# Low parts of the first stage's weight tiles: formed on GpSimd instead of VectorE

## The chip, the cores and the metric

The kernel runs on one core of a Trainium2 chip. The core has a matrix engine (TensorE, PE in the profile; its weight loads are PEld), a vector engine (VectorE, DVE), an activation engine (ScalarE, ACT), a general engine (GpSimd, POOL) and a queue engine for transfers (SyncE, SP). Each engine works through its own list of instructions in order and waits on semaphores for the others. TensorE reads from the on-chip memory SBUF and writes to the accumulators in PSUM. The metric is the time of one execution on the device in microseconds; a time is a median over runs.

## The reference

One sequence of 1024 frames with 1024 channels goes through two layers. All inputs and outputs are float32.

```
layer 0:  h = rmsnorm(x);  proj = h @ w_in                (1024 x 3328)
          14 column tiles -> RWKV-7 time mixing, 8 heads of 64 (a scan over time)
          12 column tiles -> chunked band attention, 8 heads of 64 (q, k, v)
          x += concat(y_rwkv, y_att) @ w_out
          x += square(relu(rmsnorm(x) @ up0)) @ dn0       (1024 x 4096, 4096 x 1024)
layer 1:  x += conformer_conv(rmsnorm(x))                 (pw1, GLU, causal conv of width 31,
                                                           layer norm, swish, pw2)
          x += square(relu(rmsnorm(x) @ up1)) @ dn1
output:   rmsnorm(x)
```

## The kernel before

**Products in two parts.** TensorE's fast format for float32 operands (`float32r`) keeps fewer digits than float32. So each operand is split: a high part, which is the value rounded to that format, and a low part, which is what is left. A dense product is the sum of three: high weight by high activation, high weight by low activation, low weight by high activation (lines 263, 264 and 265). ScalarE forms the high part by a copy, VectorE the low part by a subtraction of the high part from the raw value.

**Weight tiles.** `weight_part` (line 201) does this for weights. It takes a raw tile `wr` of 128 x 512 values (four blocks of 128 rows by 128 columns), loads it with a transfer on SyncE's queue (line 203), rounds it into `wh` on ScalarE (line 207) and subtracts into `wl` on VectorE (line 208). `wr` has four buffers. `wh` and `wl` have four each in the first stage (pool `wp1`) and eight each afterwards (pool `wp2`). One column tile of a product, with 1024 rows of weights, is two such parts (`weights`, line 211), and each part serves four blocks of rows, 12 matmuls of 512 columns. The value columns of the input projection (line 352) use parts of two row blocks by 256 columns: for each pair of column tiles four parts are made, and for each of four groups of frames all four are used one after the other.

**Stages.** The sequence is worked on in two halves of 512 frames. The first stage (everything before `wide[0] = True`) has: the input projection of half 0; then, mixed with one another, the scan and the attention of half 0 and the input projection of half 1; then the scan and the attention of half 1, mixed with the output projection and the feed-forward block (`up0`, `dn0`) of half 0. The second stage (after `wide[0] = True`) has the convolution of half 0, the rest of layer 0 for half 1, and the rest of layer 1 for both halves. `wide[0]` is False in the first stage and True in the second; it also makes `gemm` work on two column tiles at a time.

**Order.** The program names priorities: "support" first (loading and splitting of weights and activations, and taking results out of PSUM), then "mixer" (the scan), "attn" (the attention) and "dense" (the large matmuls). A planner at build time goes through all instructions with costs of its own, and for every engine puts the ready instruction of the highest priority next. The result is one fixed list for each engine. A change of an instruction's engine makes the planner plan anew, so other instructions can change places too. On the chip each list is worked through strictly in order.

**VectorE in the first stage.** Beside the weights' low parts it takes results out of PSUM, forms low parts of activations, and does most of the scan: among other things a triangular inversion in 16 steps of a product (line 584, two operands in SBUF) and a sum (line 587), with a detour through DRAM (`msc` to `nb`, `xsc` to `xdt`). It also does the attention's bias, maximum and scaling (lines 799 to 808).

**GpSimd before.** It sets small tiles to constants, copies a few small tiles (`dc` at line 496; the convolution's edge at lines 928 and 932), and issues transfers: stores of the projections (`pd`, `ph`, `pl`, `vd`; lines 342, 343, 345 and 371), of the mixers' outputs (`yd`; lines 719 and 828), of the half's state (`xd`, line 841), and the spreading of the bias rows (line 1055). An issue waits in GpSimd's list until the data to be stored is there.

Of the kernel before, what the change touches and what calls it, by code (L numbers as in the profile page):

```python
# [8 lines left out]
F32 = mybir.dt.float32  # L9
F32R = mybir.dt.float32r  # L10
AF = mybir.ActivationFunctionType
ALU = mybir.AluOpType
# [49 lines left out]
def encoder_trunk(ctx: ExitStack, tc: tile.TileContext, x, vecs, consts, ext, w2a2, g2, w_in, w_out,  # L62
                  up0, dn0, pw1, pw2, up1, dn1, out):
    nc = tc.nc
# [10 lines left out]
    wide = [False]  # L75
# [125 lines left out]
    def weight_part(src, n):  # L201
        raw = wpool.tile([P, KH, P], F32, tag="wr", name="wr", bufs=4)
        nc.sync.dma_start(raw[:].rearrange("p a b -> p (a b)").rearrange("p (k n) -> p k n", n=n),
                          src.rearrange("(k p) n -> p k n", p=P))
        hi = wb[0].tile([P, KH, P], F32R, tag="wh", name="wh")
        lo = wb[0].tile([P, KH, P], F32R, tag="wl", name="wl")
        nc.scalar.copy(hi[:], raw[:])  # L207
        nc.vector.tensor_tensor(out=lo[:], in0=raw[:], in1=hi[:].bitcast(F32), op=ALU.subtract)  # L208
        return hi, lo

    def weights(w, row0, m):
        return [weight_part(w[row0 + k0 * P : row0 + (k0 + KH) * P, P * m : P * m + P], P) for k0 in range(0, KT, KH)]
# [115 lines left out]
    def w_in_gemm(h, rhs, st, first=()):  # L328
# [19 lines left out]
        for n0 in range(V0 * P, V0 * P + RW, 2 * P):  # L348
            parts = []
            with boost():  # L350
                for k0 in range(0, KT, 2):
                    parts.append(weight_part(w_in[k0 * P : (k0 + 2) * P, n0 : n0 + 2 * P], 2 * P))
            for t in range(4):
                if t % 2 == 0:
                    q = psum("d")
                cs = slice(t % 2 * 2 * P, (t % 2 + 1) * 2 * P)
                ts = slice(t * P, (t + 1) * P)
                with At("dense"):
                    for k in range(KT):
                        xh, xl = rhs[k]  # L360
                        hi, lo = (a[:].rearrange("p a b -> p (a b)")[:, k % 2 * 2 * P : (k % 2 + 1) * 2 * P] for a in parts[k // 2])
                        nc.tensor.matmul(q[:, cs], xh[:, ts], hi, start=(k == 0), stop=False)
                        nc.tensor.matmul(q[:, cs], xl[:, ts], hi, start=False, stop=False)
                        nc.tensor.matmul(q[:, cs], xh[:, ts], lo, start=False, stop=(k == KT - 1))
                with boost():
                    if t % 2 == 0:
                        s = tmp("t1")
                    nc.scalar.activation(s[:, cs], q[:, cs], AF.Copy, scale=st.part[1][:, t : t + 1])
                    if t % 2:
                        r0 = h * T + (t - 1) * P  # L370
                        nc.gpsimd.dma_start(vd[r0 : r0 + 2 * P, n0 - V0 * P : n0 - V0 * P + 2 * P].rearrange("(a p) c -> p a c", p=P),
                                            s[:].rearrange("p (a c) -> p a c", a=2))
# [655 lines left out]
    with banks(d=2, w=2, v=1, c=1, a=2), tc.tile_pool(name="lop", bufs=1) as lop, tc.tile_pool(name="wp1", bufs=4) as wb[0]:  # L1028
# [5 lines left out]
        with tc.tile_pool(name="xrp", bufs=4, reuse_waits="tile") as xrp:  # L1034
            with boost():
                xa, ra, sa, first = load_x(0, xrp)
                for i, s in enumerate((slice(0, C), slice(C, P))):
                    raw = xrp.tile([P, RW], F32, tag=f"lr{i}", name="lr", bufs=1)
# [134 lines left out]
```

## Time and profile before

| what | us |
|---|---|
| median of three runs | 2561.08 (2558.75 to 2570.02) |
| the profiled execution's own time | 2570.09 |
| its span, first to last instruction | 2568.2 |
| its mean granted TensorE clock | 0.978 |
| TensorE busy (matmuls) | 2480.4 |
| VectorE busy | 1848.3 |
| ScalarE busy | 1143.9 |
| GpSimd busy | 111.6 |

All views in this document are of one profiled execution for each kernel. Times in them are counted from the first instruction. In a group's row stand the line of the program, the engine, the operation, the tile written and those read, the shape, the number of instructions, then their busy time in all, the mean duration of one in ns, and the idle time of the engine just before them with what ended it. In a row of the waits stand who waited, for whom, the time in all, how often, and the longest one. In a row on a single line of the program the durations are least, median and greatest. The chain of waits is followed back from the last instruction: at each step to what released it, or else to the instruction before it on its engine.

### The profile page before, as it was taken

The page shows a single profiled execution, that of the slowest core. Times are in us where ns is not written, and L with a number is a line of the kernel's source. Part 1 is how long each engine was busy: PE and PEld are TensorE (multiplying, and loading weights), DVE is VectorE, ACT ScalarE, POOL GpSimd, SP SyncE. Part 2 cuts the span into 40 slices and gives each one's busy share as a digit, 9 for nine tenths or more (in the row PEclk, how much of TensorE's full clock was granted, in tenths as well). Part 3 has the DMA queues.
Part 4 walks back from the last instruction along what each step waited for, and adds up shares of the span by engine and source line. Part 5 has one row for each costly group of instructions (what it writes and reads, how often), then busy time and mean ns, then how long its engine had stood idle before and what let it go on. Part 6 is the DMA issues. An engine that isn't in the chain of part 4 may idle for free.

```text
span 2568.2 us, 37380 instructions
## 1 busy us (share of the span) xinstructions
PE 2480.4 (97%) x12892; PEld 1971.0 (77%) x12892; DVE 1848.3 (72%) x3948; ACT 1143.9 (45%) x2224; POOL 111.6 (4%) x285
## 2 busy tenths in 40 slices
PE   8888999989999999999999999999999999999998
PEld 6667666757676767788888888888888888888887
DVE  5677788658788888546999974679999465544444
ACT  5345545555556655444343333533423355423324
POOL 1011001110000000000100000000000000000000
PEclk9898999989899999999999999999999999999999
DMA  8544444444333332236333333433333335333332
GB/s 266 157 141 137 115 121 119 140 130 119 95 104 107 102 101 81 77 107 197 95 93 100 96 99 99 140 115 95 95 99 99 99 91 156 95 95 98 99 97 68
DMA packets 476462, 291.24 MB, mean 113 GB/s; under 512 B 40416, under 2 KB 453472, under 8 KB 476272
## 3 DMA queue, kind: packets, MB, share of 16 engines
q1 hardware_dynamic: 466080, 258.11, 35.1%
q0 software_dynamic: 9152, 29.36, 3.3%
q8 instruction: 102, 1.67, 0.3%
q10 hardware_dynamic: 1040, 1.38, 0.2%
q14 instruction: 88, 0.72, 0.1%
HBM read 254.12 MB, written 37.77 MB: 114 GB/s over the span
## 4 chain that ended last, share of the span: by engine, by line
PE 82%; DVE 7%; DMA 6%; issue 3%; ACT 1%; SPq 0%; POOL 0%; ACTq 0%; DVEq 0%; POOLq 0%
PE d L264 23%; PE d L263 23%; PE d L265 23%; DMA nb<-msc 3%; DVE wl L208 1%; PE w L549 1%; PE a L824 1%; DVE pr L584 1%; DMA wr<-in_w_in_dram 1%; PE a L817 1%; PE c L665 1%; PE a L795 1%; DVE xi L587 1%; PE c L670 1%; DMA pt<-pd 1%
## 5 line engine op out<-in xcount | busy, mean ns | idle before, releaser
L207 ACT CAST wh<-wr 128x512 fp32r<-128x512 f32 x744 | 460.7, 621 | 988.9 <-PE d L264 897.2
L263 PE MATMUL d<-xh,wh 128*128 128x512 f32 x1872 | 748.4, 400 | 6.1 <-ACT xh L153 4.2
L264 PE MATMUL d<-xl,wh 128*128 128x512 f32 x1872 | 746.6, 399 | 0.8 <-DVE xl L154 0.4
L265 PE MATMUL d<-xh,wl 128*128 128x512 f32 x1872 | 746.3, 399 | 0.9 <-DVE wl L208 0.9
L208 DVE TENSOR_TENSOR wl<-wr,wh 128x512 fp32r<-128x512 f32 x744 | 501.9, 685 | 190.0 <-ACT wh L207 135.0
L263 PEld LDWEIGHTS d<-xh,wh 128*128 128x128 f32 x1872 | 356.9, 191 | 81.2 <-ACT xh L153 4.7
L264 PEld LDWEIGHTS d<-xl,wh 128*128 128x128 f32 x1872 | 356.5, 190 | 74.8 <-DVE xl L157 1.3
L265 PEld LDWEIGHTS d<-xh,wl 128*128 128x128 f32 x1872 | 356.5, 190 | 74.6 <-DVE wl L208 1.6
L263 PE MATMUL d<-mh,wh 128*128 128x512 f32 (+1 forms) x1040 | 405.9, 390 | 0.0
L264 PE MATMUL d<-ml,wh 128*128 128x512 f32 (+1 forms) x1040 | 405.2, 390 | 0.0
L265 PE MATMUL d<-mh,wl 128*128 128x512 f32 (+1 forms) x1040 | 404.9, 389 | 0.0
L947 DVE SCALAR_TENSOR_TENSOR cv<-u,dwt,cv 128x512 f32<-128x512 f32 x480 | 332.4, 746 | 0.7
L264 PEld LDWEIGHTS d<-ml,wh 128*128 128x128 f32 x1040 | 195.7, 188 | 38.9
L265 PEld LDWEIGHTS d<-mh,wl 128*128 128x128 f32 x1040 | 195.5, 188 | 39.1
L263 PEld LDWEIGHTS d<-mh,wh 128*128 128x128 f32 x1040 | 195.6, 188 | 38.4 <-issue 0.2
L846 DVE TENSOR_TENSOR x<-d,x 128x512 f32<-128x512 f32 (+1 forms) x146 | 97.6, 680 | 142.5 <-PE d L265 142.2
L888 DVE SCALAR_TENSOR_TENSOR t<-d,rstd 128x512 f32<-128x512 f32 x128 | 86.3, 686 | 101.2 <-PE d L265 98.1
L584 DVE TENSOR_TENSOR pr<-nb,xi 128x16 f32<-128x16 f32 (+15 forms) x256 | 101.0, 395 | 2.6
L894 DVE TENSOR_TENSOR ml<-t,mh 128x512 fp32r<-128x512 f32 x128 | 87.8, 688 | 13.5 <-ACT mh L892 10.9
L890 ACT ACTIVATE t<-t 128x512 f32<-128x512 f32 x128 | 80.1, 626 | 18.9 <-DVE t L888 18.4
L892 ACT ACTIVATE mh<-t 128x512 fp32r<-128x512 f32 x128 | 78.9, 616 | 0.0
L587 DVE TENSOR_REDUCE xi<-pr 128x8 f32<-128x16 f32 (+15 forms) x256 | 73.9, 289 | 2.4
(261 smaller groups left out, 2452.5 us busy)
## 6 DMA issues: line engine op xcount, KB each, us to landing
wr<-in_up_dram SPq DMA_DIRECT2D x256, 256.0 KB
wr<-in_dn_dram SPq DMA_DIRECT2D x256, 256.0 KB
wr<-in_w_in_dram SPq DMA_DIRECT2D x104, 256.0 KB
wr<-in_pw_dram SPq DMA_DIRECT2D x96, 256.0 KB
nb<-msc SPq DMA_DIRECT2D x16, 512.0 KB
wr<-in_w_out_dram SPq DMA_DIRECT2D x32, 256.0 KB
pd<-t POOLq DMA_DIRECT2D x28, 256.0 KB, 3.0
x<-xd SPq DMA_DIRECT2D x24, 256.0 KB
```

Source lines behind the costliest of these rows:

```text
L207: nc.scalar.copy(hi[:], raw[:])
L208: nc.vector.tensor_tensor(out=lo[:], in0=raw[:], in1=hi[:].bitcast(F32), op=ALU.subtract)
L263: nc.tensor.matmul(q[:, cols], hi, xh[:, cols], start=(k == 0), stop=False)
L264: nc.tensor.matmul(q[:, cols], hi, xl[:, cols], start=False, stop=False)
L265: nc.tensor.matmul(q[:, cols], lo, xh[:, cols], start=False, stop=(k == KT - 1))
L584: nc.vector.tensor_tensor(out=pr[:, :, :, 0:n], in0=pairs[:, r, :, 0:n].unsqueeze(2).to_broadcast([P, 2, 4, n]), in1=xi[:, :, 0:n].unsquee ...
L587: nc.vector.tensor_reduce(out=xi[:, :, n - 2 : n].rearrange("p j r -> p r j"), in_=pr[:, :, :, 0:n], op=ALU.add, axis=AX.X)
L846: nc.vector.tensor_tensor(out=xs[m][:, cols], in0=q[:, cols], in1=xs[m][:, cols], op=ALU.add)
L888: nc.vector.scalar_tensor_tensor(out=t[:], in0=q[:], scalar=0.0, in1=rstd[:], op0=ALU.max, op1=ALU.mult)
L890: nc.scalar.activation(sq[:], t[:], AF.Square)
L894: nc.vector.tensor_tensor(out=lo[:], in0=sq[:], in1=hi[:].bitcast(F32), op=ALU.subtract)
L947: nc.vector.scalar_tensor_tensor(out=c[:], in0=u[:, tap : tap + T], scalar=dw(tap), in1=c[:], op0=ALU.mult, op1=ALU.add)
```

## The change

In `weight_part` the subtraction that forms the low part is issued on GpSimd while `wide[0]` is False, that is for every weight tile of the first stage, and on VectorE afterwards, as before. Operands, shapes, buffers and priorities stay the same.

```diff
         nc.scalar.copy(hi[:], raw[:])
-        nc.vector.tensor_tensor(out=lo[:], in0=raw[:], in1=hi[:].bitcast(F32), op=ALU.subtract)
+        (nc.vector if wide[0] else nc.gpsimd).tensor_tensor(out=lo[:], in0=raw[:], in1=hi[:].bitcast(F32),
+                                                            op=ALU.subtract)
         return hi, lo
```

## The prediction

> **What bounds the kernel now.** I read the page first: its busy line, the slices and the costliest groups.
>
> ```profile
> span 2568.2 us, 37380 instructions
> PE 2480.4 (97%) x12892; PEld 1971.0 (77%) x12892; DVE 1848.3 (72%) x3948; ACT 1143.9 (45%) x2224; POOL 111.6 (4%) x285
> ...
> PE   8888999989999999999999999999999999999998
> ...
> DVE  5677788658788888546999974679999465544444
> ...
> L208 DVE TENSOR_TENSOR wl<-wr,wh 128x512 fp32r<-128x512 f32 x744 | 501.9, 685 | 190.0 <-ACT wh L207 135.0
> ...
> L584 DVE TENSOR_TENSOR pr<-nb,xi 128x16 f32<-128x16 f32 (+15 forms) x256 | 101.0, 395 | 2.6
> ```
>
> TensorE is the busy engine over the whole span, GpSimd is nearly empty, and VectorE is high in the first 18 slices, where the change lies. So I cut the first stage (to 1188 us, where the last of its dense work runs) into four stretches: all engines, then the low parts alone.
>
> ```profile
> 0.00:530.00 530.00, 483.98 (x2977) 363.24 (x2978) 385.61 (x1055) 260.06 (x571) 61.89 (x166) 0.94 0.50 148
> 530.00:580.00 50.00, 37.49 (x190) 26.30 (x189) 26.77 (x73) 24.07 (x55) 6.04 (x20) 0.80 0.48 145
> 580.00:1066.00 486.00, 465.47 (x3000) 344.16 (x2999) 396.23 (x1159) 273.48 (x596) 17.79 (x57) 0.98 0.36 98
> 1066.00:1188.00 122.00, 121.65 (x564) 99.87 (x563) 57.81 (x91) 46.68 (x78) 5.89 (x17) 1.00 0.42 123
> 0.00:1188.00 1188.00, 1108.58 (x6726) 833.57 (x6726) 866.41 (x2376) 604.30 (x1298) 91.61 (x260) 0.95 0.43 125
> ...
> 0.00:1188.00 1188.00, 169.11 (x249) 0.95 0.43 125
> ```
>
> After the length of a stretch come PE, PEld, DVE, ACT and POOL busy, the granted clock and the DMA. TensorE idles 1188 - 1108.6 = 79 us in this stage, 12.5 of it between 530 and 580, and 0.4 after 1066. Up to 1066 VectorE is busy 808.6 of 1066 us, or 76%. The last row is line 208 alone: 169 us of VectorE's 866. Its 249 instructions hold one of the next stage; by the code there are 104 + 16 + 64 + 64 = 248 (input projection, output projection, the two feed-forward matrices).
>
> Then the chain of waits of that stage, shares by line, and what TensorE waited for up to 1190 us (us in all, times, longest).
>
> ```profile
> by line: PE d L264 12.5%; PE d L263 12.4%; PE d L265 12.3%; issue 6.4%; DMA nb<-msc 6.0%; DVE wl L208 2.8%; PE w L549 2.4%; PE a L824 2.3%; DVE pr L584 2.2%; DMA wr<-in_w_in_dram 2.0%; PE a L817 1.8%; PE c L665 1.6%; PE a L795 1.5%; DVE xi
> ...
> PE v L612 <- DVE e L606: 14.3, 3, 6.3
> PE a L817 <- DVE pt L808: 7.1, 5, 3.8
> PE a L795 <- DVE yo L827: 5.9, 2, 3.5
> PE w L481 <- DVE xl L462: 5.8, 1, 5.8
> ...
> PE d L265 <- DVE wl L208: 0.9, 1, 0.9
> ```
>
> Line 208 has 2.8% of 1188 = 33 us of the chain, yet TensorE waited directly for a low part once, 0.9 us. So its cost is indirect: low parts stand in VectorE's queue ahead of the scan's and the attention's steps, for which TensorE waits (33.1 us in the four rows). That is the place where the change can pay.
>
> **The change part by part.**
>
> *Removed from VectorE:* 248 x 0.683 us (the row below) = 169 us. The same row shows VectorE idle 36.5 us before low parts, its queue held while ScalarE finishes a high part. That goes too.
>
> ```profile
> L208 DVE TENSOR_TENSOR wl<-wr,wh 128x512 fp32r<-128x512 f32 x249 | 169.6, 683 | 40.0 <-ACT wh L207 36.5 <-DMA pt<-pd 2.2 <-issue 0.4
> ...
> L422 DVE TENSOR_TENSOR e<-pt 128x256 f32<-128x256 f32 x56 | 23.4, 418 | 8.8 <-DMA pt<-pd 8.6
> ...
> L894 DVE TENSOR_TENSOR ml<-t,mh 128x512 fp32r<-128x512 f32 x32 | 22.0, 688 | 8.1 <-ACT mh L892 8.1
> ...
> L578 DVE TENSOR_TENSOR nb<-nb,fold 128x256 f32<-128x256 f32 x32 | 19.7, 617 | 0.3
> L575 DVE TENSOR_TENSOR fold<-nb 128x256 f32<-128x256 f32 x32 | 19.3, 603 | 43.0 <-DMA nb<-msc 42.8
> ```
>
> *Added to GpSimd:* 248 subtractions of 128x512 with two operands. No arithmetic of GpSimd's is in this trace; the nearest rows are memsets.
>
> ```profile
> L381 POOL MEMSET xdt<- 128x256 f32 x4 | 1.4, 344 | 0.0
> ...
> L105 POOL MEMSET ones<- 128x128 f32 x1 | 0.2, 204 | 0.3 <-POOLq L1160 0.3
> ```
>
> From 128 to 256 elements is 140 ns, 1.09 ns per element, over a fixed 64 ns. One pass over 512 elements is 0.62 us (lower end: reads and the write all overlap), three passes are 1.74 us (upper end: nothing overlaps). I take two passes, 1.18, say 1.2 us, since two operands must be read. In total 154 to 432 us, taken 298: with the 92 us that GpSimd has now, 390 of 1188. It isn't full.
>
> *What a low part's lateness costs.* A part now ends 0.7 us after its turn and would end 0.5 us later (1.1 at the upper end). In the dense stretch the distance is seen directly:
>
> ```profile
> 1092.46 0.69 DVE L208 TENSOR_TENSOR wl<-wr,wh 128x512 fp32r<-128x512 f32 x1 [1.86 <-ACT wh L207]
> ...
> 1092.29 0.39 PE L265 MATMUL d<-mh,wl 128*128 128x512 f32 x1
> 1092.51 0.39 PE L263 MATMUL d<-mh,wh 128*128 128x512 f32 x1
> ```
>
> Matmuls start 0.22 to 0.23 us apart, so a part of 4 x 3 matmuls lasts 2.7 us. With four buffers a part is started when the fourth before it is done, and three parts, some 8 us, run before it is used; less its own 0.69 that is over 7 us of cover. An extra 0.5 to 1.1 us costs nothing under it, and 1.2 us per part is under the 2.7 that a part may take. Without cover (the first part of all, and the value columns, where the four parts of a pair are used one after the other) I put +1 us in all, between 0 and 5 (four such pairs and the start, 1 us each).
>
> *The queue it joins.* GpSimd issues the stores of the projections and of both mixers, in order.
>
> ```profile
> POOL yd L828 <- DVE yo L827: 197.8, 20, 21.9
> POOL pd L345 <- DVE t L336: 141.5, 23, 37.5
> ```
>
> These waits are long because GpSimd has nothing else. Behind such a trigger a low part now waits, and behind the low part the next trigger, with the reloads (pt, and at the end mh) that wait for its data. The order is fixed by a plan, so a low part lies behind a trigger only if the plan has the trigger ready first; it is late by as much as the run strays from the plan, and TensorE's longest wait above is 6.3 us, still under 7. For the triggers I put 1.2 us of delay on the few that lie on the path: +2 us, between 0 and 6.
>
> *What it does to VectorE.* This is the term that decides. The trace has GpSimd copies of 30 elements, equal in size, that last 0.2 us alone and far more beside VectorE.
>
> ```profile
> L928 POOL COPY u<-halo x16: 208/210/1207, 1077.1 to 1511.2; 128x30 f32<-128x30 f32 x16
> ...
> 1225.49 3.79 POOL L932 COPY halo<-u 128x30 f32<-128x30 f32 x1 [9.90 <-DVE u L929]
> ...
> 1225.28 2.73 DVE L947 SCALAR_TENSOR_TENSOR cv<-u,dwt,cv 128x512 f32<-128x512 f32 x4
> 1227.93 1.29 DVE L208 TENSOR_TENSOR wl<-wr,wh 128x512 fp32r<-128x512 f32 x2
> ```
>
> The copy at 1225.49 lasts 3.79 us, to 1229.28; that is 0.06 us after the sixth of six two-operand instructions on end (the second low part ends at 1229.22). So GpSimd's reads wait while VectorE reads two operands from SBUF. I assume it holds the other way too: while a low part is formed, VectorE's two-operand instructions wait. How often? The groups shown of that kind without line 208 (L584, L422, L894, L578, L575) are 185 us, 16% of the stage; all that VectorE does besides line 208 is 697 us, 59%. So a hold of 1.2 us displaces 0.19 to 0.70 us of VectorE's work; I take the middle, 0.45 us. Against the 0.683 removed, a third of the relief is left. Below the lower end (0.62 us held, 16%) it is 0.10 us; at the upper (1.74 us, 59%) 1.03 us, and VectorE loses.
>
> The Trainium skill, SBUF — State Buffer, section "SBUF: two separate sides", calls this port pair an exclusive lock: whichever starts first keeps it for the whole instruction and the other blocks. The row of 3.79 us agrees for GpSimd's side; no row here shows VectorE blocked. Taken to the full, every hold lost, the rule would put +25 in the place of the -11 below.
>
> *Sum.* The chain's 33 us on line 208 shrink by the same third: 33 x (1 - 0.45/0.683) = -11. Of the 169 us of low parts 33, a fifth, lay on the chain; a fifth of the 36.5 us of held queue is 7, and VectorE's next step often waits for something else too, so between 0 and -7 I take -4. +1 and +2 come from above. The sum is -12 us on the profiled execution's 2570.1: 2558. This execution lies 9 us above the median of the runs, 2561.1 (2558.8 to 2570.0), so I carry the difference to the median: **2549 us**.
>
> **The rivals.**
>
> 1. *The relief counts in full.* VectorE fills GpSimd's holds with work on PSUM or on one operand. All 33 us of the chain go: 2561 - 33 = 2528. For it: the 33.1 us that TensorE waited for VectorE, and the hole at 530 to 580, where dense work has run out and waits for the last of scan and attention; a faster scan fills it. Against it: in 580 to 1066 TensorE is busy 465 of 486 us, so the dense work is right behind the chain.
>
> 2. *The port costs VectorE more than the low parts did.* Each hold of 1.2 us meets a two-operand step at its start (the inversion is one after the other) and the whole of it is lost: the chain's 33 us become 33 x 1.2/0.683 = 58, +25: 2586, slower. It decides from a mean loss of 0.683 us per part on, that is 57% of a hold of 1.2. For it: the 3.79 us row, and L584 with 256 instructions. Against it: the groups shown that need both operands from SBUF are only 16% of the stage.
>
> 3. *Nothing moves.* TensorE's dense work sets the end, and what the mixers gain they hand back as dense work after 1066, where TensorE is full: 0, 2561. For it: 97% busy. Against it: 79 us of idle time.
>
> **How the numbers follow.** What a measurement of this kernel can tell from no change is about 0.5%, 13 us. Forecast 0.45, its own range 2535 to 2570 (the ends of the lateness and queue terms, and a loss of 0.28 to 0.65 us per part, which makes the -11 anything from -19 to -2); of it 0.19 is faster by over 13 us and 0.26 within. Rival 1 has 0.20, all faster. Rival 2 has 0.22, of which 0.20 is slower. Rival 3 has 0.13. So faster 0.39, within 0.41, slower 0.20. The range of 2522 to 2584 takes in rival 1 and most of rival 2; the upper end of the hold, 1.03 us lost per part, gives +17 and lies inside.
>
> **What would show it.** Line 208 on GpSimd 248 times at about 1.2 us, and far over 1.7 if it waits for the port. VectorE's busy time to the end of the stage falls from 866 to some 700 in instructions, but those of two operands get longer on the average (L584 over 395 ns, L422 over 418) if the port blocks; if they stay, rival 1 is right. TensorE's waits for line 208 stay at a few us; if they reach tens, the cover or the queue was misjudged. The hole at 530 to 580 shrinks if the scan got faster. Everything after the stage must take the same 1380 us; if it doesn't, the reasoning by stage is wrong.

## The result and the profile after

The changed kernel takes 2642.78 us (median of four runs, 2629.33 to 2650.32) against 2559.95 us for the kernel before (four runs, 2558.75 to 2570.02): a ratio of 1.031 with an interval of 1.026 to 1.036. It is slower by 83 us. The profiled execution took 2650.32 us, the slowest of the four, as was the one before (2570.09).

In the changed kernel every line number behind the edit is higher by one (line 584 is now 585). First its page: the span, the busy times, three engines in the 40 slices, and the groups of line 208 and of the scan's inversion.

```profile
span 2648.2 us, 37367 instructions
...
PE 2518.2 (95%) x12892; PEld 1998.5 (75%) x12892; DVE 1792.2 (68%) x3700; ACT 1147.5 (43%) x2226; POOL 438.9 (17%) x533
...
PE   8788898988889989999999999999999999999998
...
DVE  4577888767878766113799994669999656534444
...
POOL 3423232332222222445110000000000000000000
...
L208 POOL TENSOR_TENSOR wl<-wr,wh 128x512 fp32r<-128x512 f32 x248 | 325.0, 1313 | 546.2 <-ACT wh L207 453.1
...
L585 DVE TENSOR_TENSOR pr<-nb,xi 128x16 f32<-128x16 f32 (+15 forms) x256 | 124.4, 486 | 3.4 <-DVE st L800 0.2
```

GpSimd does what the change says: 248 low parts of 1.31 us, 325 us, and it isn't full. The same inversion step takes VectorE 486 ns instead of 395.

Where the time went shows in windows of the two kernels, cut at the scan's last inversion step (the last start of line 584, now 585) and at the end of the first stage. The columns are those of the prediction's windows: PE, PEld, DVE, ACT and POOL busy, the granted clock, the DMA. First the kernel before:

```profile
0.00:1030.00 1030.00, 951.65 (x5919) 708.29 (x5920) 787.93 (x2228) 538.14 (x1176) 84.10 (x240) 0.95 0.44 127
1030.00:1188.00 158.00, 156.93 (x809) 125.28 (x807) 78.49 (x149) 66.16 (x123) 7.51 (x20) 1.00 0.38 111
1188.00:2568.20 1380.20, 1371.81 (x6166) 1137.44 (x6166) 981.85 (x1573) 539.62 (x927) 19.95 (x25) 1.00 0.35 104
```

And the changed kernel, with the stretch of the prediction's hole as its last row:

```profile
0.00:1019.50 1019.50, 898.39 (x5516) 660.10 (x5516) 743.06 (x1990) 508.25 (x1117) 305.24 (x408) 0.91 0.42 120
1019.50:1268.00 248.50, 247.97 (x1216) 200.43 (x1212) 67.36 (x139) 99.49 (x182) 110.32 (x100) 1.00 0.35 104
0.00:1268.00 1268.00, 1146.36 (x6726) 860.52 (x6726) 810.42 (x2128) 607.74 (x1299) 415.56 (x508) 0.93 0.40 117
1268.00:2648.20 1380.20, 1371.81 (x6166) 1137.97 (x6166) 981.79 (x1573) 539.78 (x927) 23.38 (x25) 1.00 0.35 104
530.00:580.00 50.00, 45.33 (x249) 36.19 (x248) 32.19 (x67) 19.79 (x39) 20.85 (x36) 0.91 0.61 200
```

The whole loss lies in the first stage: it ends at 1268 instead of 1188 us, and what follows takes 1380.20 us in both. In the first stage the matmuls are the same 6726, but TensorE idles 122 us instead of 79 (1268 - 1146.4) and is busy 38 us longer at a granted clock of 0.93 instead of 0.95. VectorE is busy for less time than before, 810 instead of 866 us. And yet the scan ends hardly earlier (1019.5 instead of 1030.0), with 1216 matmuls behind it instead of 809. Those run on a full TensorE (248.0 of 248.5 us), so the end of the stage is the time of that last scan step and some 0.2 us for each matmul that is left then.

What TensorE waited for in the changed kernel, up to 1290 us (the engine and line, whom it waited for, us in all, times, longest):

```profile
PE w L537 <- DVE e L534: 16.9, 7, 6.8
PE a L818 <- DVE pt L809: 15.8, 14, 4.3
PE v L613 <- DVE e L607: 11.5, 7, 4.7
PE w L482 <- DVE xl L463: 9.5, 3, 7.6
...
PE d L365 <- POOL wl L208: 1.6, 4, 0.7
...
PE d L266 <- POOL wl L208: 1.5, 3, 0.8
```

TensorE waits 3.1 us for low parts, and over 50 us for the scan's and the attention's steps on VectorE. Which of VectorE's steps got longer is seen in its groups by form up to the stage's end, first before, then after:

```profile
L494 DVE RECIPROCAL e<-dx 128x256 f32<-128x256 f32 x16 | 27.9, 1743 | 0.1
L846 DVE TENSOR_TENSOR x<-d,x 128x512 f32<-128x512 f32 x40 | 27.5, 688 | 30.1 <-PE d L265 29.9
...
L174 DVE TENSOR_TENSOR acc<-acc,t 128x512 f32<-128x512 f32 x28 | 19.2, 687 | 4.9 <-ACT t L173 4.5
...
L523 DVE TENSOR_TENSOR bk<-e 64x256 f32<-64x256 f32 x32 | 13.3, 416 | 0.4
...
L518 DVE TENSOR_SCALAR e<-e 128x256 f32<-128x256 f32 x16 | 4.5, 280 | 0.0
```

```profile
L423 DVE TENSOR_TENSOR e<-pt 128x256 f32<-128x256 f32 x56 | 28.4, 508 | 15.4 <-DMA pt<-pd 9.3 <-POOL pt L414 6.0
L495 DVE RECIPROCAL e<-dx 128x256 f32<-128x256 f32 x16 | 27.9, 1744 | 0.1
L847 DVE TENSOR_TENSOR x<-d,x 128x512 f32<-128x512 f32 x40 | 27.5, 688 | 86.7 <-PE d L266 86.5
...
L174 DVE TENSOR_TENSOR acc<-acc,t 128x512 f32<-128x512 f32 x28 | 23.4, 837 | 9.6 <-ACT t L173 9.0
...
L524 DVE TENSOR_TENSOR bk<-e 64x256 f32<-64x256 f32 x32 | 16.3, 508 | 0.5
...
L519 DVE TENSOR_SCALAR e<-e 128x256 f32<-128x256 f32 x16 | 7.1, 441 | 0.0
```

The reciprocal, with one operand, keeps its 1743 ns, and line 847, one of whose operands (`d`) is in PSUM, keeps its 688 ns (line 846 before). Line 174, with both operands in SBUF, goes from 687 to 837 ns, line 524 from 416 to 508, and line 423 from the prediction's 418 to 508. But a second tensor is not needed for a step to lengthen: line 519 multiplies and adds constants to one tile in SBUF, and it goes from 280 to 441 ns. One wait, by start and length:

```profile
291.26 3.77 POOL L208 TENSOR_TENSOR wl<-wr,wh 128x512 fp32r<-128x512 f32 x3
...
290.76 4.54 DVE L585 TENSOR_TENSOR pr<-nb,xi 128x192 f32<-128x192 f32 x1
```

One inversion step of VectorE lasts 4.54 us, to 295.30, while GpSimd forms three low parts on end, to 295.03. So VectorE's steps on two SBUF operands do wait for GpSimd's subtraction, and some of its steps on one tile too.

### The profile page after: what moved, and what is told of

Read it like the earlier page. It is cut to its first block, busy times and chain, and to the rows that moved or that the text cites. A ratio compares the mean times of both kernels' runs of the same rounds, so it can differ in the third digit from the quotient of the medians.

```text
span 2648.2 us, 37367 instructions
## 1 busy us (share of the span) xinstructions
PE 2518.2 (95%) x12892; PEld 1998.5 (75%) x12892; DVE 1792.2 (68%) x3700; ACT 1147.5 (43%) x2226; POOL 438.9 (17%) x533
## 4 chain that ended last, share of the span: by engine, by line
PE 62%; DVE 1%; ACT 0%; DMA 0%; issue 0%; SPq 0%; ACTq 0%; DVEq 0%
PE d L266 20%; PE d L264 20%; PE d L265 20%; PE o L993 0%; PE a L825 0%; DMA nb<-msc 0%; DVE pr L585 0%; PE a L796 0%; PE o L180 0%; PE w L550 0%; PE a L818 0%; DVE xi L588 0%; PE a L798 0%; PE c L678 0%; PE c L666 0%
## 5 line engine op out<-in xcount | busy, mean ns | idle before, releaser
L208 DVE TENSOR_TENSOR wl<-wr,wh 128x512 fp32r<-128x512 f32 x496 | 332.3, 685 | 149.9 <-ACT wh L207 98.7
L208 POOL TENSOR_TENSOR wl<-wr,wh 128x512 fp32r<-128x512 f32 x248 | 325.0, 1313 | 546.2 <-ACT wh L207 453.1
L585 DVE TENSOR_TENSOR pr<-nb,xi 128x16 f32<-128x16 f32 (+15 forms) x256 | 124.4, 486 | 3.4 <-DVE st L800 0.2
```

Of the source, the lines that this page charges most:

```text
L208: (nc.vector if wide[0] else nc.gpsimd).tensor_tensor(out=lo[:], in0=raw[:], in1=hi[:].bitcast(F32), op=ALU.subtract)
L585: nc.vector.tensor_tensor(out=pr[:, :, :, 0:n], in0=pairs[:, r, :, 0:n].unsqueeze(2).to_broadcast([P, 2, 4, n]), in1=xi[:, :, 0:n].unsquee ...
```

## The experiments

The edits are in `weight_part` ("half" and "late" also keep a flag outside it) and concern the first stage; afterwards low parts are on VectorE as before. Shown is what differs from the changed kernel, or from the kernel before where that is said. The open question was which part of the change costs the 83 us: the list that the planner makes without low parts on VectorE ("list"), low parts that come late ("lateness"), or what GpSimd's work does to VectorE ("port").

**None.** No low part in the first stage.

```diff
+        if not wide[0]:
+            return hi, hi
```

> First stage without any low part of the weights: the third matmul of each product reads the high part again, so the number of matmuls stays, GpSimd gets nothing, VectorE loses its 169 us. Three theories for the 83 us. Port: VectorE's two-operand steps wait on the chip while GpSimd reads, so the list of TensorE, which counts on a faster scan, is not kept. Without GpSimd's reads the scan is fast: 2520 to 2560, L585's 486 ns mean back to 395 or less. Lateness: low parts come too late from GpSimd; without them nothing is late: 2530 to 2565. List: taking work off VectorE makes the planner put fewer dense matmuls between the scan's steps, whatever GpSimd does, and the chip's scan does not get faster by it: 2620 to 2650, with some 2000 dense matmuls ahead of the last scan unit as in the changed kernel (2081), where the kernel before has 2469.

Measured: 2552.59 us against 2557.39, ratio 0.998 (0.997 to 1.000). Taking 169 us of work off VectorE without giving it to anyone is worth 5 us. The list isn't the cause either: it puts as little ahead of the scan's end as the changed kernel's does, as the page's busy line and the windows of this run show.

```profile
PE 2465.8 (97%) x12892; PEld 1966.7 (77%) x12892; DVE 1706.9 (67%) x3700; ACT 1147.1 (45%) x2226; POOL 116.3 (5%) x285
```

```profile
0.00:932.20 932.20, 858.74 (x5570) 638.98 (x5570) 660.51 (x1996) 514.06 (x1131) 85.18 (x240) 0.96 0.45 132
932.20:1168.00 235.80, 235.23 (x1158) 190.26 (x1156) 64.53 (x133) 93.74 (x170) 7.69 (x20) 1.00 0.36 106
```

The relieved scan ends 98 us earlier than before (932 against 1030), but the planner has put 349 matmuls less ahead of its end (5570 against 5919); they are done after it, on a full TensorE, in 78 us more (235.8 against 158.0). Of 98 us gained 20 are left between these two executions, and 5 between the medians.

**Unused.** GpSimd forms the low parts, and nobody reads them.

```diff
-        return hi, lo
+        return hi, (lo if wide[0] else hi)
```

> GpSimd forms all low parts of the first stage as in the changed kernel, but no matmul reads them (the third matmul reads the high part again): all port use, no lateness. Port: as slow as the changed kernel, 2625 to 2655. Lateness: 2530 to 2570. List: 2620 to 2650.

Measured: 2636.12 us against 2557.39, ratio 1.031 (1.029 to 1.032), the whole loss. Nobody waits for these low parts, so lateness is out. Its windows stand against those of "none":

```profile
0.00:999.80 999.80, 887.82 (x5505) 652.58 (x5505) 737.14 (x2002) 512.53 (x1125) 303.10 (x405) 0.91 0.42 122
999.80:1254.00 254.20, 252.41 (x1225) 203.48 (x1223) 69.78 (x128) 97.60 (x179) 114.76 (x104) 1.00 0.36 105
```

Nearly the same number of matmuls is ahead of the scan's end (5505 and 5570), but that end comes 68 us later, and the stage's end 86 us later (1254 and 1168; the 67 more matmuls left are most of the other 18). VectorE is busy 77 us longer up to the scan's end, in 6 instructions more.

**Both.** The kernel before, and beside it a subtraction on GpSimd whose result nobody reads.

```diff
         nc.vector.tensor_tensor(out=lo[:], in0=raw[:], in1=hi[:].bitcast(F32), op=ALU.subtract)
+        if not wide[0]:
+            nc.gpsimd.tensor_tensor(out=raw[:], in0=raw[:], in1=hi[:].bitcast(F32), op=ALU.subtract)
```

> The kernel before, with its low parts on VectorE, and beside it the same 248 subtractions on GpSimd, written over the raw tile after VectorE has read it; nobody reads them. Port use without any relief of VectorE. Port: VectorE's busy time in the stage grows by some 100 us over 866 and the time by 40 us or more, 2600 to 2680. Lateness: no matmul waits for GpSimd, 2555 to 2575. List: VectorE's load is that of before, so the list is too, 2555 to 2575, with about 2470 dense matmuls ahead of the last scan unit.

Measured: 2648.42 us against 2557.39, ratio 1.036 (1.034 to 1.039), 91 us. The group of GpSimd's subtraction in the page, and the windows:

```profile
L210 POOL TENSOR_TENSOR wr<-wr,wh 128x512 f32<-128x512 f32 x248 | 340.0, 1372 | 542.9 <-DVE wl L208 485.6
```

```profile
0.00:1114.40 1114.40, 991.97 (x5942) 735.88 (x5943) 912.70 (x2230) 539.14 (x1178) 365.25 (x442) 0.92 0.41 118
1114.40:1267.00 152.60, 152.09 (x785) 121.12 (x783) 87.23 (x147) 64.31 (x119) 67.56 (x66) 1.00 0.37 112
```

Here as many matmuls are ahead of the scan's end as before (5942 and 5919), and the loss is the same: the scan ends 84 us later, and the stage 79 us later. So the loss doesn't need the thin list of the relieved kernel. It comes with GpSimd's subtraction, also where VectorE is not relieved. The lists are not the same step by step, though: matching the matmuls of the first stage kind by kind, half of them stand 18 or more places from where they stood before (36 between "none" and "unused", 215 between the kernel before and the change).

**Half.** Every second part on GpSimd.

```diff
-        (nc.vector if wide[0] else nc.gpsimd).tensor_tensor(...)
+        (nc.vector if wide[0] or turn[0] % 2 else nc.gpsimd).tensor_tensor(...)
+        turn[0] += 1
```

> Every second low part of the first stage on GpSimd, the others on VectorE. If each hold of the port costs by itself (0.34 us per part, from 83 us over 248), half of the loss is left: 2590 to 2610. If the loss comes from GpSimd's queue growing long, it falls by more than half: 2560 to 2580. If any change of the lists costs it, it stays: 2625 to 2655.

Measured: 2593.95 us against 2559.74, ratio 1.014 (1.009 to 1.018), 34 us, as a cost that grows with the number of holds asks.

**Copy.** GpSimd copies the raw tile into the low part: one operand in place of two.

```diff
+            nc.gpsimd.tensor_copy(lo[:], raw[:])
```

> As the changed kernel, but GpSimd copies the raw tile into the low part instead of subtracting (the low parts are then not what they should be): one operand read instead of two, so a hold of 0.6 to 0.8 us instead of 1.3. Port: the loss falls with the hold, about half of the 83 us, 2590 to 2610. Lateness: half or less, 2560 to 2600. List: no better than the changed kernel, 2620 to 2650.

Measured: 2564.22 us against 2557.39, ratio 1.003 (1.001 to 1.005), 7 us. For the port I expected some half of the loss, and it is a twelfth. (The time lies in the range given for lateness, which "unused" rules out.) The copy holds GpSimd half as long, but VectorE waits far less than half of 85 us (1720.5 - 1706.9 = 14 us over "none"). The page's busy line and the group of the copy:

```profile
PE 2469.1 (97%) x12892; PEld 1967.2 (77%) x12892; DVE 1720.5 (67%) x3700; ACT 1145.2 (45%) x2226; POOL 274.4 (11%) x533
...
L211 POOL CAST wl<-wr 128x512 fp32r<-128x512 f32 x248 | 160.8, 650 | 602.0 <-PE d L268 375.5
```

**Copy2 and pieces.** This miss left open whether the length of GpSimd's instruction counts or its second operand. Copy2 makes two copies for each part; pieces makes the subtraction in four instructions of 128 elements.

```diff
+            nc.gpsimd.tensor_copy(lo[:], raw[:])
+            nc.gpsimd.tensor_copy(lo[:], hi[:].bitcast(F32))
```

> GpSimd makes two copies per part, of the raw tile and then of the high part, in the place of the subtraction (the low parts are then not what they should be): GpSimd's time per part is that of a subtraction, about 1.3 us, but each copy reads one operand. Port, by the wait of VectorE: twice that of one copy (17 us) and so 2565 to 2590. Queue: if GpSimd's stores, which wait behind the parts, are what costs, the time is that of the changed kernel: 2625 to 2650.

Measured: 2585.29 us against 2559.74, ratio 1.010 (1.006 to 1.013), 26 us, as expected for the port and far from the queue's range.

```diff
+            for a in range(KH):
+                nc.gpsimd.tensor_tensor(out=lo[:, a, :], in0=raw[:, a, :], in1=hi[:, a, :].bitcast(F32), op=ALU.subtract)
```

> All low parts of the first stage on GpSimd, each in four subtractions of 128 elements instead of one of 512. If a hold lasts for one instruction, VectorE gets in between them and waits a quarter as long for each: 2570 to 2610, and the longest two-operand step of VectorE is below 2 us, where L585's longest is 4.5 us now. If only GpSimd's reading time counts, the loss stays: 2630 to 2660.

Measured: 2623.47 us against 2559.74, ratio 1.023 (1.019 to 1.028), 64 us, between the two expectations. The longest inversion step (line 588 there) lasts 2.06 us and a two-operand step of line 579 2.38, over the 2 us expected, where the changed kernel has 4.54. The groups of GpSimd's work in the two pages, with the busy line of pieces; copy2 first:

```profile
L211 POOL CAST wl<-wr 128x512 fp32r<-128x512 f32 x248 | 159.4, 644 | 481.7 <-PE d L269 397.4
L212 POOL CAST wl<-wh 128x512 fp32r<-128x512 f32 x248 | 161.4, 653 | 29.1 <-ACT wh L207 16.0
```

```profile
PE 2493.7 (96%) x12892; PEld 1977.9 (76%) x12892; DVE 1754.1 (67%) x3700; ACT 1143.1 (44%) x2224; POOL 591.4 (23%) x1277
...
L212 POOL TENSOR_TENSOR wl<-wr,wh 128x128 fp32r<-128x128 f32 x992 | 475.3, 509 | 395.0 <-ACT wh L207 357.8
```

Copy2 keeps GpSimd at work for as long as the subtraction does (321 against 325 us) and costs under a third of it. So neither the hold's time nor GpSimd's stores waiting behind it is the price by itself; an instruction with two operands costs VectorE more. Pieces are at work longer in all (475 us) and cost less than the whole subtraction: short holds help, but don't make it free.

**Late.** GpSimd only for the last two of the four groups of the feed-forward block, 64 parts, where most of the scan is past.

```diff
-        (nc.vector if wide[0] else nc.gpsimd).tensor_tensor(...)
+        (nc.gpsimd if late_low[0] else nc.vector).tensor_tensor(...)
...
+            late_low[0] = not wide[0] and grp >= 2
```

> Low parts on GpSimd only for the last two of the four groups of the feed-forward block (64 of 248 parts), on VectorE before that. The lists are those of the kernel before up to the last scan unit; some 20 of the 64 parts are formed while the scan still runs. If each part costs 0.34 us wherever it is formed: +21, 2573 to 2585. If it costs only where the scan runs: +7 at most, 2552 to 2568.

Measured: 2568.83 us against 2559.74, ratio 1.004 (1.002 to 1.005), 9 us: just over the edge of "only beside the scan", and under half of the 21 us that an even share would be. Of the 64 parts 12 start before the scan's last inversion step, where some 20 were expected.

**High.** A version that might be faster: the kernel before, but the high parts of the first stage copied on GpSimd instead of ScalarE, since a copy had cost only 7 us.

```diff
-        nc.scalar.copy(hi[:], raw[:])
+        if wide[0]:
+            nc.scalar.copy(hi[:], raw[:])
+        else:
+            nc.gpsimd.tensor_copy(hi[:], raw[:])
```

> The kernel before, but with the high parts of the first stage copied on GpSimd instead of ScalarE: one operand read, some 0.65 us per part, 248 parts, and ScalarE loses 248 x 0.62 = 154 us. If GpSimd's one-operand reads cost what the single copy showed (17 us of VectorE's waiting and +7 us), and relief of an engine off the bound is worth as little as taking 169 us off VectorE was (-5): 2555 to 2572, no version that beats the kernel before. If ScalarE's relief shortens the scan where TensorE waits for it: 2535 to 2552.

Measured: 2589.28 us against 2556.84, ratio 1.013 (1.011 to 1.016), 32 us slower. It is outside both expectations. VectorE, which forms the low parts from these high parts, now waits for GpSimd, as the row of its waits shows:

```profile
DVE wl L211 <- POOL wh L210: 43.1, 52, 2.7
```

But before, it waited 36.5 us for ScalarE at the same place (the prediction's row of line 208), so this is only some 7 us more. Why the same copy costs 32 us here and 7 us in "copy" is not shown.

Here is all of it in one table. VectorE's waiting is its busy time over the whole span less that of a kernel with the same VectorE instructions: "none" (1706.9 us) for those with 3700, the kernel before (1848.3 us) for those with 3948 (of "both", 1981.9; of "high", 1874.2; of "copy2", 1740.1; of "unused", 1788.3). For "half" and "late", which have no such partner, it is the sum over all VectorE instructions of the trace but the low parts, up to the convolution, less the same sum for "none" (by this sum the copy's waiting is 17 us, the number in the later expectations). The last column is the difference of the medians.

| kernel | GpSimd's holds | VectorE waits, us | slower than before, us |
|---|---|---|---|
| none | none | 0 | -5 |
| late | 64 of 1.29 us | 10 | 9 |
| copy | 248 of 0.65 us, one operand | 14 | 7 |
| high | 248 of 0.71 us, one operand | 26 | 32 |
| copy2 | 496 of 0.65 us, one operand | 33 | 26 |
| pieces | 992 of 0.51 us | 47 | 64 |
| half | 124 of 1.34 us | 49 | 34 |
| unused | 248 of 1.32 us | 81 | 79 |
| the change | 248 of 1.31 us | 85 | 83 |
| both | 248 of 1.37 us | 134 | 91 |

In "late", "copy", "copy2", "unused" and the change the loss lies within 7 us of VectorE's waiting. "High" and "pieces" seem to lose more than they wait, but the waits are those of one execution, in both the fastest of four: by its own time (2584.36 and 2609.44 us) "high" loses 28 us for 26, "pieces" 50 for 47. "Both" and "half" lose less than they wait.

The price per hold hides where it is paid. Here are GpSimd's low parts of the changed kernel ahead of the scan's last inversion step and behind it (after the length: VectorE's and GpSimd's time on line 208, the clock, the DMA):

```profile
0.00:1019.50 1019.50, 0.00 (x0) 221.80 (x168) 0.91 0.42 120
1019.50:1268.00 248.50, 0.09 (x1) 103.19 (x80) 1.00 0.35 104
```

Comparing the duration of each VectorE step other than a low part with the mean of the same step in the kernel before and in "none", 86 of 87 us of waiting lie ahead of that step. So a low part cost VectorE 0.5 us (86 over 168) while the scan ran and next to nothing behind it; 0.34 is the mean of both. The same count gives 0.5 in "unused" (80 us over 165) and in "half" (48 over 92), and in "late" 8 us over the 12 parts ahead and 2 over the 52 behind. In "both", where 46 of the 248 are formed behind the scan's last inversion step, those cost 12 us, so behind it isn't always nothing.

## Why the prediction was wrong

The forecast was 2549 us, faster by a little. It is slower by 83 us, outside the range.

**Right.** The duration of a hold: 1.31 us against 1.2 taken, inside the bounds. Two passes also fit the medians of 0.46 us for 128 elements ("pieces") and 1.29 us for 512: 2.16 ns per element, twice the 1.09 of the memsets. The fixed part is then 0.18 us and not 0.06. The cover of low parts: TensorE waited 3.1 us for them, and "unused" shows that their lateness costs nothing. What comes after the stage: 1380.2 us in both. The port blocks VectorE, though not only in steps with two operands in SBUF, and the size was fairly right: 85 us over 248 holds is 0.34 us per low part, where 0.45 was taken. By that, half of the 0.683 us would have been left to gain, not a third. That 0.45 is near is partly luck, for it was the middle of a wide range, 0.19 to 0.70, and was meant for every part alike. The Trainium skill, SBUF — State Buffer, section "SBUF: two separate sides", has the one that comes second fully blocked. The 4.54 us row shows VectorE blocked, but not that order: its step is recorded as starting 0.50 us before the first of the three low parts.

**The step that failed** is the sum's main term: "The chain's 33 us on line 208 shrink by the same third". It set the relief and the waits off against one another, as if a microsecond of VectorE were worth the same in both. They have different prices.

- The relief is worth almost nothing. "None" has all of it, 169 us, with no waits, and gains 5 us. The share of 33 us that line 208 had in the chain of waits wasn't time to be had: where the planner takes the low parts off VectorE, it brings the scan forward and leaves more dense work behind it. That is rival 3, "what the mixers gain they hand back as dense work after 1066", and it had 0.13.
- A wait for the port cost about as much as it lasted in most of these kernels. In "both" and "unused" about as many matmuls are ahead of the scan's end as in the kernel without the waits (5942 for 5919, 5505 for 5570), the scan's last step comes 84 and 68 us later, and the stage's end follows it by 79 and 86 us. The likely reason is that in a fixed list the dense work that could fill the gap stands behind the late matmul: TensorE idles (122 us instead of 79), and its granted clock is lower too (0.93 instead of 0.95 over the stage).

So the sum should have been 0 to -5 for the relief and 248 x 0.45 = +112 for the waits with the prediction's own number, or +84 with the measured one. Both are slower by far. The direction is rival 2's (0.22), but not its condition: it decided only "from a mean loss of 0.683 us per part on", again by the netting, and its +25 was too small for the same reason.

**The other terms.** The hole at 530 to 580 did shrink (TensorE is busy 45.3 us there instead of 37.5, with 249 matmuls instead of 190), although the scan is hardly faster: it was no sign of a faster scan, since the changed list has other work there. VectorE's busy time fell to 810 us and not to some 700: without any low part it is 725 ("none", its two windows together), and the other 85 are the waits. The held queue (-4) is part of the relief, which is 5 us in all; the triggers (+2) weren't tried by themselves, but "copy2" keeps the queue occupied as long and loses 26 us in all, so they can hardly be more than that.

What the planner counts was not looked into; that it leaves the port out is concluded from the number of matmuls ahead of the scan's end, which is alike with GpSimd's subtraction and without. That the delay passes to the end because of the fixed list fits most of the ten kernels, but no run gave VectorE the same waits without GpSimd, and every run has a list planned anew, so a part of each loss can be the list's. Of the 80 us in the stage 42 are idle time and 38 are longer matmuls at a lower clock; whether the second part follows wholly from the first was not tried. Why "both" loses only 91 us with 134 us of waits, and "half" 34 with 49, is open.

## What to carry to other kernels

Before work is moved off an engine, ask what a planned relief of it is worth, and price the new waits by themselves: where an order is planned and TensorE sets the end, planned time on another engine can be worth nothing while unplanned time on a serial chain counts nearly in full. A share in the chain of waits is no time to be had, least of all where the planner plans anew. On GpSimd, an elementwise step of 1.3 us with two operands cost VectorE some 0.5 us of waiting here where it worked on the scan, and far less behind it.

## What the runs showed of the hardware

- Most of the waits are those of VectorE's steps with two operands in SBUF: lines 174, 423 and 524 lengthen by a fifth, while the reciprocal (1743 and 1744 ns) and a sum with one operand in PSUM (688 ns) don't. But steps on one SBUF tile can wait too: line 519, a multiplication and addition of constants, goes from 280 to 441 ns in the mean. Such steps and VectorE's copies have some 13 of the 87 us.
- I had not expected that the kind of GpSimd's instruction counts more than its time. For 248 low parts VectorE waited 85 us beside 325 us of two-operand subtractions, but 33 us beside 321 us of copies and 14 us beside 161 us of copies. By the section of the Trainium skill named above, what starts first keeps the port for its whole instruction, whichever kind it is; by length alone both kinds would then cost alike. Measured, the price for the same length differs by a factor of 2.6, and no run here shows why.
- A VectorE step can be held through several of GpSimd's instructions: the row of 4.54 us began 0.50 us before the first of three low parts on end and finished 0.27 us after the last. Its earlier start in the trace gave it no precedence.
- Two-operand subtractions on GpSimd take 1.31 us in the mean for 512 elements a partition and 0.51 for 128 ("pieces"); a copy of 512 takes 0.65 ("copy").
